# Two accumulating transfers in place of four behind each seven-product unit, and buffer pools of 34 and 34

## The chip, the cores and the metric

The kernel runs on one core of a Trainium2 chip. The metric is the device time of one execution in microseconds (us), the median of several runs. Names of engines: PE is TensorE (matmuls), DVE is VectorE, ACT is ScalarE, POOL is GpSimd, which here issues DMAs, and SP is SyncE, which issues the weight loads. PEld are TensorE's weight loads.

## The reference

One layer of an encoder on 512 tokens of width 2048, all in float32:

```
h = rmsnorm(x); proj = h @ w_in
attn   = mixture_of_dilations(q, k, v)          # 16 heads, three dilated windows
gla    = chunked gated linear attention, forward + backward, norm, swish gate
x = x + concat(attn, gla) @ w_out
h = rmsnorm(x)
x = x + (silu(h @ w_gate) * (h @ w_up)) @ w_down   # hidden width 5632
return rmsnorm(x) * final_norm_w
```

What matters here are the matrix products with `w_in` (its query and key columns), `w_gate` and `w_up`.

## The kernel before

Every float32 operand is cut into two parts, hi (a cast to fp32r) and lo (the difference to the original), and a product is the sum of hi·hi, hi·lo and lo·hi. The products with `w_gate` and `w_up` (class `Feed`, the feed-forward stage) and with the query and key columns of `w_in` (class `Front`, the front stage, which inherits from it) go by a scheme with seven products in place of eight for a 2 x 2 block product. A *unit* is 256 columns of one weight; `Feed` has 44 units (gate and up in turn), `Front` 8. A unit runs in four *pieces* (q = 0 to 3) of the contraction, and each piece needs:

- a raw weight tile, loaded by SyncE (`read`, L1366), at most three ahead;
- block sums of it on VectorE (`sums`, L1385 to L1387);
- two casts on ScalarE (`split`, L1398: one of 768 columns from the raw tile, one of 1024 from the sums) and two differences on VectorE (L1403);
- 28 matmuls on TensorE (`products`, L1480 and L1494) into seven banks of PSUM.

The pieces are prepared about one piece ahead: the loop `run` calls `split(i + 1)` ahead of `products(i)`. After the fourth piece `evac7` takes the seven banks m1, t2, t1, t3, m2, t4, b22 out of PSUM. The first halves are combined on VectorE into the tile c (L1514 and L1515, the names of the small helpers `add` and `sub`); the second halves are copied by ScalarE (L1520 to L1528) into r1, r2, r3, and after the addition at L1538 (which the profile shows at the helper's line, L1514, with 128x512 elements) GpSimd issues four DMAs that add them into c. The transfers overlap in c's columns, so the third and fourth wait until the first two have landed. `finish` then multiplies c on VectorE (L1578 for gate, L1585 for up, L1637 in the front stage), some pieces later. The first two units of `Feed` use another scheme (`evac`) without such transfers, so 42 + 8 units have them.

Buffers come from two pools: s2 with tiles of 512 columns (2 KB in each of 128 partitions) and s4 with tiles of 1024 columns. Each pool hands out the slot that was given back longest ago (`Slots`, a queue). Everything is given out when the program is built; at run time an instruction that writes a slot waits for the last users of that slot. On each engine the instructions run in the order in which the program lists them. `KEEP_X`, `KEEP_F` and `MOST_4` say how many operands go to which pool.

Of the kernel before, what the change touches and what calls it, by code (L numbers as in the profile page):

```python
# [15 lines left out]
F32 = mybir.dt.float32  # L16
# [3 lines left out]
OP = mybir.AluOpType  # L20
# [3 lines left out]
P = 128  # L24
# [9 lines left out]
BIG = 1e30  # L34
LINE = 1024
BIASW = 896
KEEP_X, KEEP_F, MOST_4 = 5, 2, 18

C_AQ, C_AK, C_AV = 0, 1024, 2048
C_GQ, C_GK, C_GV, C_GR, C_LR = 3072, 3584, 4096, 5120, 6144  # L40

N2 = 36
N4 = 33

# [66 lines left out]
def put(*slots):  # L113
    for s in slots:
        if s.home is not None:
            s.home.free.append(s.i)


def layer(nc, tc, x, attn_norm_w, w_in, rel_table, gw_f, gb_f, gw_b, gb_b, gla_norm_w, w_out,
# [3 lines left out]
    w_gate, w_up, w_down, out = w_gate[0], w_up[0], w_down[0], out[0]  # L123
    pe, act, dve, pool, sp = nc.tensor, nc.scalar, nc.vector, nc.gpsimd, nc.sync
    mm = pe.matmul

    with tc.manual_schedule(), \
# [4 lines left out]
            tc.tile_pool(name="ps", bufs=1, space=PSUM, reuse_waits="tile") as pp:  # L132
        s2 = Slots(p2, N2, 512, "a")
        s4 = Slots(p4, N4, 1024, "b")
        ps = Slots(pp, 8, 512, "ps")
# [44 lines left out]
        class Stream:  # L180
# [14 lines left out]
            def add(self, pieces):  # L195

                for segs in pieces:
                    self.pieces.append([segs, None])
                    for h in range(2):
                        self.halves.append([len(self.pieces) - 1, h, None, None])  # L200
# [1208 lines left out]
        class Feed(Blocks):  # L1409
# [100 lines left out]
            def evac7(self, u, banks):  # L1510


                a, z = slice(0, 256), slice(256, 512)
                add = lambda o, x_, y_: dve.tensor_tensor(o, x_, y_, op=OP.add)  # L1514
                sub = lambda o, x_, y_: dve.tensor_tensor(o, x_, y_, op=OP.subtract)  # L1515
                c_ = s4.get(F32, [P, 2, 512])
                c = c_.t.rearrange("p f t -> p (f t)")
                m1, t2, t1, t3, m2, t4, b22 = (b.t for b in banks)
                t, v, r1, r2, r3 = (s2.get() for _ in range(5))
                act.copy(t.t[:, a], m1[:, a])  # L1520
                act.copy(r3.t[:, a], t1[:, z])
                act.copy(r2.t[:, z], t1[:, z])
                act.copy(r3.t[:, z], t3[:, z])
                act.copy(r1.t[:, a], m2[:, z])
                act.copy(c[:, 512:768], t4[:, a])
                act.copy(r2.t[:, a], t4[:, z])  # L1526
                act.copy(c[:, 256:512], b22[:, a])
                act.copy(r1.t[:, z], b22[:, z])  # L1528
                add(t.t[:, a], t.t[:, a], m1[:, z])
                sub(t.t[:, z], t.t[:, a], t2[:, a])  # L1530
                sub(t.t[:, z], t.t[:, z], t2[:, z])
                add(v.t[:, a], t1[:, a], t.t[:, z])
                add(v.t[:, z], t3[:, a], t.t[:, z])
                add(c[:, 768:1024], t1[:, a], v.t[:, z])
                add(c[:, a], m2[:, a], t.t[:, a])
                put(*banks)
                yield
                add(c[:, 256:768], c[:, 256:768], v.t)  # L1538
                put(t, v)
                pool.dma_start(out=c[:, 0:512], in_=r1.t, accum_op=OP.add)  # L1540
                pool.dma_start(out=c[:, 512:1024], in_=r2.t, accum_op=OP.add)
                pool.dma_start(out=c[:, 256:768], in_=r3.t, accum_op=OP.add)
                pool.dma_start(out=c[:, 768:1024], in_=r3.t[:, z], accum_op=OP.add)
                put(r1, r2, r3)
                for _ in range(3 if u < len(self.units) - 2 else 7):
                    yield
                yield from self.finish(u, c_, c)
# [601 lines left out]
```

## Time and profile before

| | |
|---|---|
| time, median of 3 runs | 2184.84 us (2183.32 to 2185.92) |
| span of the profiled execution | 2184.5 us |
| busy PE / DVE / ACT / POOL | 99% / 81% / 55% / 16% |
| granted TensorE clock | 0.999 |
| TensorE's share of the chain that ended last | 87% |
| DMA | 397.81 MB, mean 182 GB/s |

The profile is of one execution. Its page lists busy time for each engine, groups of instructions by line, and DMA issues with the time to landing. In a row of a timeline stand the start, the duration, the engine, the line, the operation, the tiles written and read (a is s2, b is s4, ps a PSUM bank) and, in brackets, the time for which the engine was idle before, with what ended that. A row of waits gives the engine that waited, the one that released it, the total in us, how many times, and the longest.

### The profile page before, as it was taken

How to read it: one execution, taken by the hardware profiler on the slowest of the kernel's cores; microseconds unless marked ns; L12 is line 12 of the kernel's file. 1: busy time of each engine (PE TensorE's matmuls, PEld its weight loads, DVE VectorE, ACT ScalarE, POOL GpSimd, SP SyncE). 2: the span in 40 equal slices, each digit the busy share in tenths (PEclk: the TensorE clock that was granted, in tenths of full speed). 3: DMA queues.
4: the chain of work that ended last, by engine and by line, in shares of the span. 5: the costliest groups of instructions: out<-in, count | busy, mean ns of one | idle time of the engine just before them, and what ended most of it. 6: DMA issues, size and time to landing. Idle time of an engine off the chain costs nothing.

```text
span 2184.5 us, 34570 instructions
## 1 busy us (share of the span) xinstructions
PE 2163.5 (99%) x12618; PEld 1904.8 (87%) x12618; DVE 1770.9 (81%) x3072; ACT 1195.3 (55%) x2190; POOL 338.8 (16%) x474
## 2 busy tenths in 40 slices
PE   9999999999999999999999999999999999999998
PEld 7888778888888888988888888888888899999986
DVE  5699867776677557899999899998999888898885
ACT  7454456776654335555555555555555655555562
POOL 0012231110101110012212122121221220021300
PEclk9999999999999999999999999999999999999999
DMA  6367784543337873377767777767776975576982
GB/s 191 125 182 176 184 240 131 179 142 105 116 97 255 293 261 107 116 186 176 194 174 184 184 176 193 176 183 184 176 194 176 264 195 181 184 182 157 283 305 78
DMA packets 256856, 397.81 MB, mean 182 GB/s; under 512 B 18925, under 2 KB 154269, under 8 KB 256686
## 3 DMA queue, kind: packets, MB, share of 16 engines
q1 hardware_dynamic: 201406, 272.49, 39.1%
q0 software_dynamic: 54960, 122.58, 24.9%
q8 instruction: 99, 1.62, 0.3%
q14 instruction: 71, 0.58, 0.1%
q10 hardware_dynamic: 320, 0.53, 0.1%
HBM read 285.37 MB, written 64.29 MB: 160 GB/s over the span
## 4 chain that ended last, share of the span: by engine, by line
PE 87%; issue 6%; DMA 3%; DVE 2%; ACT 1%; POOL 0%; DVEq 0%; ACTq 0%; SPq 0%; POOLq 0%
PE ps L1494 26%; PE ps L1480 13%; PE ps L346 6%; PE ps L347 6%; PE ps L348 6%; PE ps L1850 5%; PE ps L1851 5%; PE ps L1849 5%; DMA b<-a 3%; PE ps L339 3%; PE ps L337 3%; PE ps L338 3%; PE ps L651 1%; PE ps L1075 1%; PE ps L619 1%
## 5 line engine op out<-in xcount | busy, mean ns | idle before, releaser
L1398 ACT CAST b<-b 128x768 fp32r<-128x768 f32 (+1 forms) x537 | 489.2, 945 | 337.4 <-DVE b L1403 150.0
L1403 DVE TENSOR_TENSOR b<-b,b 128x768 fp32r<-128x768 f32 (+1 forms) x537 | 564.0, 1084 | 33.9 <-ACT b L1398 21.9
L1494 PE MATMUL ps<-b,b 128*128 128x512 f32 x1552 | 451.2, 393 | 0.4 <-ACT b L1398 0.2
L1494 PE MATMUL ps<-a,b 128*128 128x512 f32 x1248 | 366.0, 394 | 3.3 <-DVE b L1514 3.3
L1494 PEld LDWEIGHTS ps<-b,b 128*128 128x128 f32 x1552 | 263.6, 189 | 30.6 <-ACT b L1398 0.7
L1480 PEld LDWEIGHTS ps<-b,b 128*128 128x128 f32 x1552 | 252.9, 190 | 36.0
L1480 PE MATMUL ps<-b,b 128*128 128x256 f32 x1552 | 275.9, 281 | 0.0
L1480 PEld LDWEIGHTS ps<-a,b 128*128 128x128 f32 x1248 | 208.0, 189 | 34.1 <-DVE b L1403 0.4
L1494 PEld LDWEIGHTS ps<-a,b 128*128 128x128 f32 x1248 | 207.3, 189 | 23.4 <-ACT a L1526 4.0
L1480 PE MATMUL ps<-a,b 128*128 128x256 f32 x1248 | 223.9, 281 | 0.0
L1385 DVE TENSOR_TENSOR b<-b 128x512 f32<-128x512 f32 x244 | 167.4, 686 | 20.1 <-DMA b<-in_w_down_dram 6.7
L1850 PE MATMUL ps<-b,b 128*128 128x256 f32 x624 | 176.9, 284 | 0.0
L1851 PE MATMUL ps<-b,b 128*128 128x256 f32 x624 | 176.9, 284 | 0.0
L1849 PE MATMUL ps<-b,b 128*128 128x256 f32 x624 | 176.9, 284 | 0.0
L346 PE MATMUL ps<-b,b 128*128 128x512 f32 x352 | 140.7, 400 | 2.0 <-ACT b L237 2.0
L347 PE MATMUL ps<-b,b 128*128 128x512 f32 x352 | 138.4, 393 | 0.9 <-DVE b L218 0.9
L348 PE MATMUL ps<-b,b 128*128 128x512 f32 x352 | 138.2, 392 | 0.0
L1851 PEld LDWEIGHTS ps<-b,b 128*128 128x128 f32 x624 | 119.9, 192 | 0.0
L1849 PEld LDWEIGHTS ps<-b,b 128*128 128x128 f32 x624 | 119.9, 192 | 0.0
L1850 PEld LDWEIGHTS ps<-b,b 128*128 128x128 f32 x624 | 119.9, 192 | 0.0
L218 DVE TENSOR_TENSOR b<-b,b 128x512 fp32r<-128x512 f32 x144 | 96.5, 687 | 24.0 <-ACT b L237 23.9
L1387 DVE TENSOR_TENSOR b<-b,b 128x256 f32<-128x256 f32 x244 | 103.8, 426 | 8.4
(294 smaller groups left out, 4352.2 us busy)
## 6 DMA issues: line engine op xcount, KB each, us to landing
b<-in_w_gate_dram SPq DMA_DIRECT2D x109, 512.0 KB, 4.1
b<-in_w_up_dram SPq DMA_DIRECT2D x88, 512.0 KB, 3.8
b<-in_w_down_dram SPq DMA_DIRECT2D x88, 512.0 KB, 6.6
b<-in_w_in_dram SPq DMA_DIRECT2D x78, 512.0 KB, 4.2
b<-a POOLq DMA_DIRECT2D x150, 256.0 KB, 4.5
b<-in_w_out_dram SPq DMA_DIRECT2D x32, 512.0 KB, 6.6
gd<-b POOLq DMA_DIRECT2D x22, 512.0 KB, 3.9
b<-gd SPq DMA_DIRECT2D x22, 512.0 KB, 5.7
```

Source lines behind the costliest of these rows:

```text
L346: mm(o, xh.t[:, c], wh.t[:, w], start=first and not on, stop=False, skip_group_check=on)
L347: mm(o, xh.t[:, c], wl.t[:, w], start=False, stop=False, skip_group_check=on)
L348: mm(o, xl.t[:, c], wh.t[:, w], start=False, stop=last, skip_group_check=on)
L1385: dve.tensor_tensor(s_[:, :, 0:2], r[:, :, 1:3], r[:, :, 0:1].to_broadcast(shape), op=OP.add)
L1387: dve.tensor_tensor(s_[:, :, 3], s_[:, :, 2], r[:, :, 3], op=OP.add)
L1398: act.copy(o, src)
L1403: dve.tensor_tensor(o, src, h, op=OP.subtract)
L1480: mm(o, wl, xh, start=False, stop=end, skip_group_check=True)
L1494: mm(o.rearrange("p (s t) -> p s t", s=2), wh, x_, start=first and p == 0, stop=False, skip_group_check=True)
L1849: mm(o, xh[:, t], wh, start=first and h == 0, stop=False, skip_group_check=True)
L1850: mm(o, xh[:, t], wl, start=False, stop=False, skip_group_check=True)
L1851: mm(o, xl[:, t], wh, start=False, stop=last, skip_group_check=True)
```

## The change

The copies of the second halves go into two s4 tiles, r with 1024 columns and g with 768, in place of three s2 tiles. r is added to all of c by one transfer and g to columns 256 to 1023 by a second, which waits for the first. For that the second half of t3 is copied twice into g by one instruction that reads it with a stride of zero. The pools change from 36 and 33 slots to 34 and 34 (the same memory), `KEEP_X` from 5 to 2 and `MOST_4` from 18 to 19. From L1520 on, lines of the changed kernel stand one lower or higher: the two transfers are its L1541 and L1542, and the stages behind them are one line earlier.

```diff
-KEEP_X, KEEP_F, MOST_4 = 5, 2, 18
+KEEP_X, KEEP_F, MOST_4 = 2, 2, 19
...
-N2 = 36
-N4 = 33
+N2 = 34
+N4 = 34
...
                 m1, t2, t1, t3, m2, t4, b22 = (b.t for b in banks)
-                t, v, r1, r2, r3 = (s2.get() for _ in range(5))
+                t, v = s2.get(), s2.get()
+                r, g = s4.get(), s4.get(F32, [P, 768])
                 act.copy(t.t[:, a], m1[:, a])
-                act.copy(r3.t[:, a], t1[:, z])
-                act.copy(r2.t[:, z], t1[:, z])
-                act.copy(r3.t[:, z], t3[:, z])
-                act.copy(r1.t[:, a], m2[:, z])
+                act.copy(g.t[:, 0:256], t1[:, z])
+                act.copy(r.t[:, 768:1024], t1[:, z])
+                act.copy(g.t[:, 256:768].rearrange("p (i c) -> p i c", i=2), t3[:, None, z].to_broadcast([P, 2, 256]))
+                act.copy(r.t[:, 0:256], m2[:, z])
                 act.copy(c[:, 512:768], t4[:, a])
-                act.copy(r2.t[:, a], t4[:, z])
+                act.copy(r.t[:, 512:768], t4[:, z])
                 act.copy(c[:, 256:512], b22[:, a])
-                act.copy(r1.t[:, z], b22[:, z])
+                act.copy(r.t[:, 256:512], b22[:, z])
...
                 add(c[:, 256:768], c[:, 256:768], v.t)
                 put(t, v)
-                pool.dma_start(out=c[:, 0:512], in_=r1.t, accum_op=OP.add)
-                pool.dma_start(out=c[:, 512:1024], in_=r2.t, accum_op=OP.add)
-                pool.dma_start(out=c[:, 256:768], in_=r3.t, accum_op=OP.add)
-                pool.dma_start(out=c[:, 768:1024], in_=r3.t[:, z], accum_op=OP.add)
-                put(r1, r2, r3)
+                pool.dma_start(out=c, in_=r.t, accum_op=OP.add)
+                pool.dma_start(out=c[:, 256:1024], in_=g.t, accum_op=OP.add)
+                put(r, g)
```

## The prediction

> **What bounds the kernel now.** I read the page first, then the stretches of the feed-forward stage, then the waits of TensorE, and then the timelines of VectorE, ScalarE and GpSimd through two units.
>
> ```profile
> span 2184.5 us, 34570 instructions
> PE 2163.5 (99%) x12618; PEld 1904.8 (87%) x12618; DVE 1770.9 (81%) x3072; ACT 1195.3 (55%) x2190; POOL 338.8 (16%) x474
> 1000.00:1019.50 19.50, 19.50 (x114) 17.12 (x113) 17.07 (x27) 10.10 (x18) 4.02 (x5) 1.00 0.77 211
> 1019.50:1039.00 19.50, 19.50 (x114) 17.12 (x113) 17.99 (x29) 11.35 (x20) 3.51 (x4) 1.00 0.65 154
> PE ps L1494 <- DVE b L1514: 3.3, 4, 1.8
> ```
>
> TensorE is busy for 99% of the span, and in the two stretches (two units, a gate and an up unit) it has no pause; so the kernel runs at TensorE's pace. The columns after the length are PE, PEld, DVE, ACT and POOL busy. VectorE is second: 17.07 and 17.99 of 19.50 us, so it can be stopped for about 1.5 to 2.4 us in a unit before it sets the pace itself. The last row is TensorE's longest kind of wait in the front stage (125 to 288 us): 3.3 us for banks that the evacuation frees late. That is what a better evacuation could win.
>
> **The unit's loop.** The change touches the four accumulating transfers. Their rows for one unit, then their landing times over the 41 units between 920 and 1710 us, and the count of units in the front stage:
>
> ```profile
> 1004.32 0.86 POOL L1540 DMA_DIRECT2D b<-a  x1 [3.83 <-PE ps L1480]
> 1004.87 1.22 POOL L1541 DMA_DIRECT2D b<-a  x1
> 1010.60 0.87 POOL L1542 DMA_DIRECT2D b<-a  x1 [4.51 <-issue]
> 1011.14 1.21 POOL L1543 DMA_DIRECT2D b<-a  x1
> ...
> L1540 POOL DMA_DIRECT2D b<-a x41: 857/862/905, 927.7 to 1706.3; - x41
> ...
> L1541 POOL DMA_DIRECT2D b<-a x41: 1188/1200/1234, 928.3 to 1706.9; - x41
> DMA to landing us min/median/max: 4.3/5.3/11.1
> ...
> L1543 POOL DMA_DIRECT2D b<-a x40: 872/1208/1230, 934.1 to 1694.3; - x40
> DMA to landing us min/median/max: 3.9/5.4/7.1
> ...
> L1540 POOL DMA_DIRECT2D b<-a x7: 862/862/899, 135.6 to 259.1; - x7
> ```
>
> From first to last issue, a unit takes (1706.3 - 927.7) / 40 = 19.47 us, a pair 38.93; in the front stage (259.1 - 135.6) / 6 = 20.58 us.
>
> Before, r1, r2, r3 lie in s2 slots that only the next unit's evacuation takes again. After, r and g lie in s4, from which every cast (L1398), difference (L1403) and weight load takes its buffers in turn. The listing of the changed program's instructions shows who gets them. Its instruction order on TensorE, VectorE, ScalarE and SyncE is as before; only the tiles and the waits differ:
>
> ```
> 205 L1541 DMACopy b0_833_9821<-b2_834_9824 128x1024
> 206 L1542 DMACopy b0_833_9821<-b28_835_9825 128x768
> 1004 L1398 TensorCopy b2_849_9942<-b11_832_9791 128x768 [waits DMAHW0_49,DMASW5_49]
> 1005 L1398 TensorCopy b28_850_9943<-b14_842_9896 128x1024 [waits DMASW6_49,DVE_49]
> 208 L1542 DMACopy b8_860_10020<-b1_862_10024 128x768 [waits DMASW7_49]
> 1448 L1385 TensorTensor b21_875_10138<-b17_868_10054 128x2x256 [waits DMAHW6_49,DMASW7_49]
> 1023 L1398 TensorCopy b1_876_10142<-b31_859_9990 128x768 [waits DMAHW5_49,DMASW0_49]
> ```
>
> The number after b is the slot. Slot 28 was g of one unit; the second cast for piece 3 of the next unit writes it, so that cast waits until g has landed. In the other kind of unit (g in slot 1) it is the first cast. These two kinds take turns through the whole feed-forward stage; the front stage has the second kind in all but its last unit. VectorE's difference reads the cast, and behind it in VectorE's order stand the rest of the casts' differences, the evacuation, and the addition after which the next r may start. This is a closed loop, and its time is the unit's time once it exceeds 19.47 us.
>
> **Its length, from rows.** The addition, the difference that will wait, and the next addition, for the two kinds and for the front stage; the two casts; and VectorE's waits for others between 1009.6 and 1042.6 us and, last row, between 181.4 and 195.6 us:
>
> ```profile
> 1003.07 0.69 DVE L1514 TENSOR_TENSOR b<-b,a 128x512 f32<-128x512 f32 x1
> 1009.59 1.22 DVE L1403 TENSOR_TENSOR b<-b,b 128x1024 fp32r<-128x1024 f32 x1
> 1022.57 0.69 DVE L1514 TENSOR_TENSOR b<-b,a 128x512 f32<-128x512 f32 x1
> 1028.22 0.95 DVE L1403 TENSOR_TENSOR b<-b,b 128x768 fp32r<-128x768 f32 x1
> 1042.70 0.69 DVE L1514 TENSOR_TENSOR b<-b,a 128x512 f32<-128x512 f32 x1
> ...
> 181.40 0.95 DVE L1403 TENSOR_TENSOR b<-b,b 128x768 fp32r<-128x768 f32 x1
> 195.63 0.69 DVE L1514 TENSOR_TENSOR b<-b,a 128x512 f32<-128x512 f32 x1
> ...
> 1008.71 0.84 ACT L1398 CAST b<-b 128x768 fp32r<-128x768 f32 x1 [1.23 <-PE ps L1480]
> 1009.70 1.05 ACT L1398 CAST b<-b 128x1024 fp32r<-128x1024 f32 x1 [0.16 <-DVE b L1403]
> ...
> DVE a L1514 <- ACT a L1520: 1.7, 1, 1.7
> DVE a L1514 <- PE ps L1480: 0.5, 2, 0.3
> DVE b L1585 <- DMA b<-a: 0.5, 1, 0.5
> DVE b L1403 <- PE ps L1480: 0.2, 1, 0.2
> ...
> DVE a L1514 <- ACT a L1522: 1.2, 1, 1.2
> ```
>
> *The transfers.* No row shows an accumulating transfer of 1024 or 768 columns, so they are bounded by the pairs with the same bytes. Pair one, from first issue to last landing: 0.55 (1004.87 - 1004.32) + 5.3 = 5.85 us in the median, 0.55 + 4.3 = 4.85 at best. Pair two: 0.55 + 5.4 = 5.95, or 4.45. Between them lies one step of GpSimd, which I take from addition's end to issue: 1004.32 - 1003.76 = 0.56. So the chain is 12.36 us if the merged transfers take what the pairs' medians take. At best it is 9.86, less the two second issues of 0.55, 8.76. Nothing speaks for an end (less contention at a slower pace, but twice the bytes in each packet), so I take the middle, 10.56. With the step ahead of r, g lands G = 11.12 us after the addition ends.
>
> *VectorE behind it.* First kind: from 1009.59 to the next addition's end at 1023.26, 13.67 us; second kind: 1028.22 to 1043.39, 15.17. Of these 28.84 us, 2.9 were waits for others, which a late VectorE no longer meets: 25.94 remain. With the cast that waits ahead of each (1.05 and 0.84) a pair takes 2G + 27.83 = 50.07 us in place of 38.93. G lands 5.3 and 6.2 us after the difference's old start (5.83 and 4.96 us after the addition), far over VectorE's room.
>
> *The sum.* The feed-forward stage has 42 such units; the first is not held up, so 41 are, 20.5 pairs: 20.5 x 11.14 = 228 us. The front stage: 14.92 us (181.40 to 196.32) - 1.2 + 0.84 + 11.12 = 25.68 in place of 20.58, in 7 of its 8 units: 7 x 5.10 = 36 us. Total 2184.5 + 228 + 36 = **2448 us**. The profiled execution's 2184.5 stands within 0.4 us of the median of the runs shown (2184.84), so no correction is due. At a chain of 8.76 the same sum gives 2362, at 12.36 it gives 2535.
>
> *The rest, priced at nothing.* A hundred fewer issues by GpSimd (0.86 to 1.22 us each) shorten no chain, since GpSimd is 16% busy. The front stage's 3.3 us of bank waits are inside the old 20.58 and so gone already in the new period. One copy out of a bank is 512 columns wide in place of 256:
>
> ```profile
> L1524 ACT COPY a<-ps 128x256 f32<-128x256 f32 x2 | 0.7, 373 | 0.6 <-PE ps L1480 0.6
> L1582 ACT ACTIVATE b<-b 128x512 f32<-128x512 f32 x2 | 1.2, 636 | 0.0
> ```
>
> At most 0.636 - 0.373 = 0.26 us, hidden by ScalarE's waits while VectorE is late; without that cover 50 x 0.26 = 13 us. KEEP_X and MOST_4 move operands between pools without adding instructions. Weight loads in the front stage now take the slot of a stored result and wait for that store, with SyncE's later loads queued behind. They have to be there for block sums, which wait for r's landing anyway; without this cover, some 1 us in each of 7 units.
>
> **The rivals.**
>
> *Merging pays more.* Plain transfers of 512 KB issued by GpSimd:
>
> ```profile
> gd<-b POOLq DMA_DIRECT2D x22, 512.0 KB, 3.9
> qkd<-b POOLq DMA_DIRECT2D x8, 512.0 KB, 3.1
> ```
>
> If a merged transfer landed in 3.9 or 3.1 us like these, the chain would be 8.36 or 6.76 us, the pair 45.67 or 42.47, the front unit 23.48 or 21.88, and the time 2343 or 2266: about 2305. Against it: in the best pair, 512 KB accumulated took 4.85. The page "DMA: Bandwidth & Descriptors" of the Trainium skill (section "Anatomy of one DMA") speaks for it: it fits a GpSimd transfer as 2.0 us plus bytes at 436 GB/s, an estimate of 3.2 and 2.9 us here, and so 2261 us.
>
> *TensorE restarts slowly.* In the new loop it would stand still some 25.0 - 19.5 = 5.5 us in each unit. At the kernel's start, between 6 and 16 us, the same matmul took longer than on average:
>
> ```profile
> L346 PE MATMUL ps<-b,b 128*128 128x512 f32 x5 | 3.3, 663 | 2.0 <-ACT b L237 2.0
> L346 PE MATMUL ps<-b,b 128*128 128x512 f32 x352 | 140.7, 400 | 2.0 <-ACT b L237 2.0
> ```
>
> Some eight slow ones by 0.26 us after each pause are 2.1 us; half would reach the evacuation, 1 us in 48 units: 2496. Against it: TensorE has the 5.5 us to make it up, and the granted clock in the stretches read 1.00. The page "TensorE: Matmul & The Clock Gate" (Part 1) of the Trainium skill says that an idle window of about 3.4 us halves the clock until a busy one has passed; no pause in this trace is that long (the longest in the row above is 1.8).
>
> *Faster.* If the slots came round late enough, the casts would not wait; only the front stage's 3.3 us would go: 2181. It decides at 2G + 27.83 = 38.93, G = 5.55, a chain under 4.99 us. Pair one alone needed 4.85 at best, so two transfers cannot fit.
>
> **How the numbers follow.** The loop as summed 0.76, a shorter chain 0.12, slow restarts 0.08, faster 0.03, and 0.01 for no change by casts that wait without holding VectorE. Slower than by 0.2% (4.4 us, about what a measurement of this kernel can tell) are the first three: 0.96. The range takes in the sum's bounds and the upper half of the shorter chain: 2335 to 2535.
>
> **What would show it.** Right: ScalarE at L1398 waits for the DMA of b, 3 to 8 us in every unit; VectorE at L1403 waits for it; TensorE is busy near 80% between 930 and 1700 us; first issues lie 25 us apart. The chain's term is read from L1541's and L1542's landings. Wrong: casts that start as before, or landings near 3.1 us, which put the time near 2266.

## The result, and the profile after

The changed kernel took **2498.08 us** in the median (2490.17 to 2502.15), the kernel before 2184.84 (2183.32 to 2185.92): a ratio of **1.143**, with a 95% interval of 1.1416 to 1.144. The forecast was 2448 us, with a range of 2335 to 2535.

First the page of the changed kernel: its span, the busy times, the granted clock in 40 slices (9 is 90% or more), and of its DMA issues those of r, g and the store of gate's result, with KB each and the median us to landing.

```profile
span 2497.6 us, 34239 instructions
PE 2285.8 (92%) x12618; PEld 1967.8 (79%) x12618; DVE 1772.1 (71%) x3072; ACT 1196.2 (48%) x2190; POOL 249.6 (10%) x374
...
PEclk9998899999999999989889898898888999999999
...
b<-b POOLq DMA_DIRECT2D x50, 512.0 KB, 6.2
b<-b POOLq DMA_DIRECT2D x50, 384.0 KB, 4.8
...
gd<-b POOLq DMA_DIRECT2D x22, 512.0 KB, 5.4
```

VectorE and ScalarE did the same work as before (1770.9 and 1195.3 us), and GpSimd less (338.8 before). TensorE shows 122 us more of busy time with the same instructions: matmuls that ran slower, of which more below. The rest of the 313 us is idle time, and the waits of the changed kernel say for what:

```profile
ACT b L1398 <- DMA b<-b: 513.4, 68, 13.4
POOL b L1541 <- DVE b L1385: 381.8, 25, 19.1
...
POOL b L1542 <- DMA b<-b: 287.1, 49, 9.3
DVE b L1403 <- ACT b L1398: 271.4, 85, 6.5
PE ps L1494 <- ACT b L1398: 177.0, 58, 7.6
...
DVE b L1385 <- DMA b<-b: 73.5, 24, 5.1
```

Read them as a ring: GpSimd starts g's transfer (L1542) when r has landed, ScalarE's casts wait for the transfers (`DMA b<-b`), VectorE waits for the casts, and GpSimd waits for VectorE before it can issue the next r. (The profile infers who released a wait: for r it mostly names L1385 or L1398, but in the timeline below each r is issued 0.6 us behind the end of the addition, L1514.) That TensorE's 177 us of waiting for casts are a consequence, two of the runs below test. Before, the casts' longest wait was for VectorE, and TensorE's waits were a few us.

Two units of the changed kernel in its timelines, a few instructions of GpSimd, ScalarE and VectorE (start, duration, engine, line, operation, tiles, and the idle time before it with what ended that); the rows between them are left out:

```profile
1493.49 0.68 DVE L1514 TENSOR_TENSOR b<-b,a 128x512 f32<-128x512 f32 x1
1494.81 0.86 POOL L1541 DMA_DIRECT2D b<-b  x1 [3.89 <-ACT b L1398]
1502.71 0.83 ACT L1398 CAST b<-b 128x768 fp32r<-128x768 f32 x1 [8.05 <-DMA b<-b]
1502.97 0.87 POOL L1542 DMA_DIRECT2D b<-b  x1 [7.31 <-DMA b<-b]
1507.02 2.73 ACT L1398 CAST b<-b 128x1024 fp32r<-128x1024 f32 x3 [3.47 <-DMA b<-b]
1508.09 3.23 DVE L1403 TENSOR_TENSOR b<-b,b 128x1024 fp32r<-128x1024 f32 x3 [3.56 <-ACT b L1398]
1512.47 0.59 ACT L1524 COPY b<-ps 128x512 f32<-128x512 f32 x1 [0.34 <-PE ps L1480]
1518.89 0.69 DVE L1514 TENSOR_TENSOR b<-b,a 128x512 f32<-128x512 f32 x1
1520.19 0.87 POOL L1541 DMA_DIRECT2D b<-b  x1 [16.35 <-DVE b L1385]
1525.85 0.69 DVE L1385 TENSOR_TENSOR b<-b 128x512 f32<-128x512 f32 x1 [2.75 <-DMA b<-b]
1526.11 0.86 POOL L1542 DMA_DIRECT2D b<-b  x1 [5.05 <-DMA b<-b]
1530.12 3.46 ACT L1398 CAST b<-b 128x768 fp32r<-128x768 f32 x4 [9.33 <-DMA b<-b]
...
1544.25 0.69 DVE L1514 TENSOR_TENSOR b<-b,a 128x512 f32<-128x512 f32 x1
```

Both kinds of unit are there, in turn. In the first, a cast starts when r has landed (1502.71) and the next when g has (1507.02). In the second, the block sums start when r has landed (1525.85) and a cast when g has (1530.12). From addition to addition it is 25.40 and 25.36 us here.

The changed kernel's line L1541, over the feed-forward stage (41 units) and over the front stage (7 units): issue durations in ns (least, median, most), first and last start, and the time to landing.

```profile
L1541 POOL DMA_DIRECT2D b<-b x41: 860/862/900, 978.5 to 2013.8; - x41
...
DMA to landing us min/median/max: 5.1/6.1/9.9
...
L1541 POOL DMA_DIRECT2D b<-b x7: 856/862/899, 137.0 to 302.7; - x7
...
DMA to landing us min/median/max: 5.5/6.3/8.0
```

A feed-forward unit takes (2013.8 - 978.5) / 40 = 25.88 us in place of 19.47, a front unit (302.7 - 137.0) / 6 = 27.62 in place of 20.58. 41 x 6.41 + 7 x 7.04 = 312 us, and the spans differ by 2497.6 - 2184.5 = 313.1. So the loss is all in these units.

### The profile page after: what moved, and what is told of

It reads as the page before. It is cut to its first block, busy times and chain, and to the rows that moved or that the text cites. A ratio compares the mean times of both kernels' runs of the same rounds, so it can differ in the third digit from the quotient of the medians.

```text
span 2497.6 us, 34239 instructions
## 1 busy us (share of the span) xinstructions
PE 2285.8 (92%) x12618; PEld 1967.8 (79%) x12618; DVE 1772.1 (71%) x3072; ACT 1196.2 (48%) x2190; POOL 249.6 (10%) x374
## 4 chain that ended last, share of the span: by engine, by line
PE 25%; DMA 12%; DVE 10%; issue 8%; ACT 3%; POOL 1%; DVEq 0%; ACTq 0%; POOLq 0%
DMA b<-b 12%; PE ps L1494 4%; PE ps L1849 4%; PE ps L1848 4%; PE ps L1850 4%; DVE b L1403 4%; ACT b L1398 3%; PE ps L1480 2%; DVE b L1385 1%; PE ps L346 1%; PE ps L347 1%; PE ps L348 1%; DVE b L1514 1%; DVE a L1514 1%; DVE b L1584 1%
## 5 line engine op out<-in xcount | busy, mean ns | idle before, releaser
L1398 ACT CAST b<-b 128x768 fp32r<-128x768 f32 (+1 forms) x537 | 479.8, 942 | 738.4 <-DMA b<-b 513.4
L1403 DVE TENSOR_TENSOR b<-b,b 128x768 fp32r<-128x768 f32 (+1 forms) x537 | 564.4, 1085 | 274.9 <-ACT b L1398 271.4
L1494 PE MATMUL ps<-a,b 128*128 128x512 f32 x1248 | 422.2, 443 | 145.6 <-ACT b L1398 145.6
L1494 PE MATMUL ps<-b,b 128*128 128x512 f32 x1552 | 459.9, 399 | 31.4 <-ACT b L1398 31.4
L1494 PEld LDWEIGHTS ps<-a,b 128*128 128x128 f32 x1248 | 235.6, 215 | 175.9 <-ACT b L1398 156.4
L1494 PEld LDWEIGHTS ps<-b,b 128*128 128x128 f32 x1552 | 269.4, 193 | 62.3 <-ACT b L1398 33.0
L1480 PEld LDWEIGHTS ps<-a,b 128*128 128x128 f32 x1248 | 233.1, 216 | 88.7 <-DVE b L1403 54.4
L1480 PEld LDWEIGHTS ps<-b,b 128*128 128x128 f32 x1552 | 256.5, 193 | 40.6 <-DVE b L1403 3.8
L1480 PE MATMUL ps<-b,b 128*128 128x256 f32 x1552 | 280.4, 284 | 0.5 <-DVE b L1403 0.5
L1480 PE MATMUL ps<-a,b 128*128 128x256 f32 x1248 | 261.7, 314 | 11.9 <-DVE b L1403 10.9
L1385 DVE TENSOR_TENSOR b<-b 128x512 f32<-128x512 f32 x244 | 167.7, 687 | 124.6 <-DMA b<-b 73.5
L1849 PE MATMUL ps<-b,b 128*128 128x256 f32 x640 | 181.3, 283 | 0.0
L1850 PE MATMUL ps<-b,b 128*128 128x256 f32 x640 | 181.3, 283 | 0.0
L1848 PE MATMUL ps<-b,b 128*128 128x256 f32 x640 | 181.3, 283 | 0.0
L346 PE MATMUL ps<-b,b 128*128 128x512 f32 x380 | 153.4, 404 | 9.1 <-ACT b L237 9.1
L347 PE MATMUL ps<-b,b 128*128 128x512 f32 x380 | 150.5, 396 | 0.9 <-DVE b L218 0.9
L348 PE MATMUL ps<-b,b 128*128 128x512 f32 x380 | 150.2, 395 | 0.0
L1848 PEld LDWEIGHTS ps<-b,b 128*128 128x128 f32 x640 | 123.0, 192 | 0.0
L1849 PEld LDWEIGHTS ps<-b,b 128*128 128x128 f32 x640 | 123.0, 192 | 0.0
L1850 PEld LDWEIGHTS ps<-b,b 128*128 128x128 f32 x640 | 123.0, 192 | 0.0
L218 DVE TENSOR_TENSOR b<-b,b 128x512 fp32r<-128x512 f32 x154 | 103.4, 686 | 19.6 <-ACT b L237 19.6
```

The lines of the kernel that those rows point to most:

```text
L346: mm(o, xh.t[:, c], wh.t[:, w], start=first and not on, stop=False, skip_group_check=on)
L347: mm(o, xh.t[:, c], wl.t[:, w], start=False, stop=False, skip_group_check=on)
L348: mm(o, xl.t[:, c], wh.t[:, w], start=False, stop=last, skip_group_check=on)
L1385: dve.tensor_tensor(s_[:, :, 0:2], r[:, :, 1:3], r[:, :, 0:1].to_broadcast(shape), op=OP.add)
L1398: act.copy(o, src)
L1403: dve.tensor_tensor(o, src, h, op=OP.subtract)
```

## Experiments

Each ran beside the kernel before, which had medians of 2185.55 to 2186.20 us in these comparisons. *Theory* is the loop: casts and sums that take r's and g's buffers wait for the landing, and in-order engines carry the delay round to the next r. A figure in the expectations, 11.53 us from r's issue to g's landing, is a mean over 41 units; the last of them, behind which other work runs, is an outlier, and without it the mean is 11.37.

**Give r and g back two steps later.** The transfers stay two; only the place at which the buffers return to the pool moves, so that other tiles take them later.

```diff
-                put(r, g)
-                for _ in range(3 if u < len(self.units) - 2 else 7):
+                for n in range(3 if u < len(self.units) - 2 else 7):
+                    if n == 2:
+                        put(r, g)
                     yield
```

> The changed kernel with r and g given back two steps of the evacuation later (two pieces later), so that the free queue hands their slots out only after g has landed; the transfers stay as they are. Slot theory (the time comes from casts that wait for g's landing because they were given its slot): every such wait goes and the time comes back to 2178 to 2192 us, TensorE near 99% busy in the stage. Transfer theory (the two large accumulating transfers themselves slow the core, by contention or by a late result): they are all still there, so 2450 to 2500 us.

Measured: 2200.42 us, ratio 1.0063 (1.0048 to 1.0078). r's issues and landings in that run, and then two of the waits that are left in it:

```profile
L1541 POOL DMA_DIRECT2D b<-b x41: 860/862/900, 926.5 to 1720.2; - x41
...
DMA to landing us min/median/max: 4.6/5.7/9.9
```

```profile
PE ps L1494 <- DVE b L1514: 12.1, 15, 1.8
...
ACT b L1522 <- DMA b<-b: 46.5, 16, 4.5
```

298 of the 313 us are gone, with the merged transfers and the pools of 34 and 34 in place; r lands only little sooner. The place of giving back is the cause. The 8 us above the expected range are not all explained; the two waits shown, for banks and for a slot that a transfer still reads, are among what is left.

**One step later.** The same edit with `n == 1`.

> As the changed kernel, with r and g given back one step later: g's slot now goes to a cast of the next unit's first piece (in place of its predecessor's fourth), whose difference stands some 2.2 us (first kind of unit) and 3.5 us (second kind and front stage) later in VectorE's order. Slot theory, by the same loop sum with the chain as measured after the change (11.4 us in the mean, GpSimd's step 0.28): pair 2 x 11.68 + 1.89 + 20.15 = 45.4 us in place of 38.93, front unit 23.2 in place of 20.58, so 2184 + 133 + 18 = 2335 us (2310 to 2365). If a wait for g cost the same wherever it stands: 2498. If only the fourth piece's wait mattered: 2185.

Measured: 2338.36 us, ratio 1.0702 (1.0679 to 1.0724). r's issues in that run, and its longest wait of the casts:

```profile
L1541 POOL DMA_DIRECT2D b<-b x41: 860/864/902, 952.8 to 1862.0; - x41
```

```profile
ACT b L1398 <- DMA b<-b: 262.6, 66, 8.6
```

(1862.0 - 952.8) / 40 = 22.73 us for a unit, so 45.46 for a pair where the loop's sum gave 45.4. The loss shrinks in steps with the place of giving back, as the theory has it.

**Leave g's transfer out.** The result then lacks g's addend; the casts still wait for r.

```diff
                 pool.dma_start(out=c, in_=r.t, accum_op=OP.add)
-                pool.dma_start(out=c[:, 256:1024], in_=g.t, accum_op=OP.add)
```

> The changed kernel with g's transfer left out (its 768 columns are missing from c); the copies into g stay, and r's transfer and all slots stay. Slot theory: g's slots have no late reader, only r's remain; r lands 6.4 us after the addition. First kind of unit: the fourth piece's first difference comes 2.3 us late, of which VectorE's 2.0 us of waits hide most; second kind: block sums 2.95 us late, 1.0 hidden; front 1.75 net. 20.5 x 2.25 + 7 x 1.75 = 58, so 2243 us (2220 to 2265). Transfer theory: with 384 of 896 KB gone, 43% of the loss goes: 2364 us.

Measured: 2292.21 us, ratio 1.0487 (1.0472 to 1.0503): between the two forecasts, and above the theory's range. r's issues and landings in that run:

```profile
L1541 POOL DMA_DIRECT2D b<-b x41: 853/864/897, 949.4 to 1819.2; - x41
...
DMA to landing us min/median/max: 4.7/7.2/9.4
```

The theory had r land 6.4 us after the addition ends. In the mean it was 7.33 here and 8.17 in the front stage (worked out from the trace), 0.93 and 1.77 later. With that the expectation's sum gives a pair 2.25 + 2 x 0.93 = 4.11 us more than before and a front unit 1.75 + 1.77 = 3.52: 20.5 x 4.11 + 7 x 3.52 = 109 us, and 2184.5 + 109 = 2293.5 where the span is 2294.5. That was worked out afterwards. This made the landing time the open question.

**Less work for TensorE.** In the middle pieces of each seven-product unit 28 half-wide matmuls (lo·hi) are left out. The expectation speaks of the 42 units of the feed-forward stage, but the front stage takes `products` from the same class, so all 50 units lose them: the page counts 11218 matmuls in place of 12618, 1400 fewer.

```diff
-                            rest.append((o[:, 0:256], wl, xh, end))
+                            if not together:
+                                rest.append((o[:, 0:256], wl, xh, end))
```

> The changed kernel with the lo-hi matmuls of the two middle pieces left out in the 42 seven-product units of the feed-forward stage (that part of the product is missing): 28 matmuls of 256 columns fewer in a unit, 3.4 us of TensorE's work at its full pace. If VectorE's loop through g sets the unit's time, TensorE only waits longer: 2480 to 2500 us. If TensorE's slow restarts (granted clock 0.944) set it, or any part of its work is in the loop, the time falls by up to 42 x 3.4 = 143: 2355 us.

Measured: 2558.78 us, ratio 1.1703 (1.1685 to 1.172). Less work, and 61 us *more* than the changed kernel, outside what either side had expected. r's issues (L1542 there) and landings in that run, and TensorE's wait:

```profile
L1542 POOL DMA_DIRECT2D b<-b x41: 860/864/900, 982.4 to 2076.1; - x41
...
DMA to landing us min/median/max: 5.8/8.2/9.9
```

```profile
PE ps L1494 <- ACT b L1398: 389.7, 70, 10.5
```

TensorE only waits longer, so its work does not set the pace. What changed is the landing: r takes 8.2 us. More weight loads ran beside it: in the 6 us behind r's issue their queue moved 1050 KB in the mean of the 41 units, against 823 KB in the changed kernel (worked out from the traces). Why the loads moved there is not shown; slots that TensorE gives up sooner, so that loads into them start sooner, would do it.

**More work for TensorE.** The same 28 matmuls are issued twice, again in all 50 units (14018 matmuls); the kernel then computes another result.

```diff
                     for o, wl, xh, end in rest:
+                        if together:
+                            mm(o, wl, xh, start=False, stop=False, skip_group_check=True)
                         mm(o, wl, xh, start=False, stop=end, skip_group_check=True)
```

> The changed kernel with more work for TensorE: each of the 28 half-wide matmuls (256 columns) that the middle pieces of a feed-forward unit put last is issued twice (the output is another one). At 0.12 us each that is 3.4 us per unit. Theory (the loop through the slots sets the pace, TensorE has slack): nothing is added, the period stays at 25 to 26 us, 2498 us (2440 to 2515); with less TensorE work the transfers had landed later and the time had grown by 60 us, so a fall below 2498 would fit. Rival (TensorE's own work, or its slow restarts, set the pace): 41 x 3.4 = 139 us more, 2637 us (2600 to 2660).

Measured: 2520.58 us, ratio 1.1526 (1.1506 to 1.1545). At the expectation's 0.12 us each, the 1400 matmuls are 168 us of work (its 139 us counted 41 units of the feed-forward stage alone), and they cost 22. That is 6 us above the theory's range and 79 below the rival's. r's issues (L1543 there) and landings in that run, and TensorE's wait:

```profile
L1543 POOL DMA_DIRECT2D b<-b x41: 860/862/900, 977.5 to 2028.8; - x41
...
DMA to landing us min/median/max: 4.5/6.9/9.5
```

```profile
PE ps L1496 <- ACT b L1398: 66.3, 28, 3.6
```

The extra work went into TensorE's waits for casts (66.3 us are left of 177.0). What it cost came by the landing: 6.9 us for r, and in the feed-forward stage 0.39 us more from the addition to g's landing (the table below).

**Four transfers in the changed kernel's buffers.**

```diff
-                pool.dma_start(out=c, in_=r.t, accum_op=OP.add)
-                pool.dma_start(out=c[:, 256:1024], in_=g.t, accum_op=OP.add)
+                pool.dma_start(out=c[:, 0:512], in_=r.t[:, 0:512], accum_op=OP.add)
+                pool.dma_start(out=c[:, 512:1024], in_=r.t[:, 512:1024], accum_op=OP.add)
+                pool.dma_start(out=c[:, 256:768], in_=g.t[:, 0:512], accum_op=OP.add)
+                pool.dma_start(out=c[:, 768:1024], in_=g.t[:, 512:768], accum_op=OP.add)
```

> The changed kernel with its buffers (r and g among the slots that casts and sums reuse, given back at once), but with the four accumulating transfers of before (512 columns each) instead of two. Theory (the loop through the slots): the time hangs on the time from the first issue to the last landing; in the feed-forward stage of the kernel before, four transfers took 12.39 us on average and the two of the changed kernel 11.53 us, so each unit gets about 0.9 us longer: 2498 + 48 x 0.9 = 2541 us (2510 to 2580). Rival (merged transfers are what is slow): with four transfers the kernel goes back to 2185 to 2300 us.

Measured: 2563.48 us, ratio 1.1727 (1.1702 to 1.1752). The first issues of that run's units:

```profile
L1541 POOL DMA_DIRECT2D b<-b x41: 860/862/905, 983.0 to 2068.4; - x41
```

So the merging is not what is slow: in the same loop, four transfers cost 65 us more than two, (2068.4 - 983.0) / 40 = 27.14 us for a unit against 25.88.

**More traffic on the DMA engines.** Behind each weight load of these units (and of the first two of the feed-forward stage), SyncE also copies half of the tile to a place that nothing reads. This asks what makes r and g land later than the sum had it.

```diff
+        ex, extra = dr.tile([256, P, 512], F32, name="ex"), []
...
                              in_=w[k * P:(k + n_kt) * P, col:col + n].rearrange("(k p) c -> p k c", p=P))
+                if not isinstance(self, Down):
+                    sp.dma_start(out=ex[len(extra)].rearrange("p (k c) -> p k c", k=2),
+                                 in_=w[k * P:(k + 2) * P, col:col + n].rearrange("(k p) c -> p k c", p=P))
+                    extra.append(i)
```

> The changed kernel, and SyncE issues behind each weight load of the seven-product units (and of their first two) a copy of half of that weight tile (256 KB) to a place in the chip's memory that nothing reads. No instruction of TensorE, VectorE, ScalarE or GpSimd changes. It asks why the two transfers of r and g took longer from first issue to last landing (11.53 us on average in the feed-forward stage) than the 10.56 us of the sum. Theory (the weight loads that are under way take a share of the DMA engines): in the changed kernel r's landing grew by about 0.45 us per 100 KB of weight loads in the 6 us behind its issue, 824 KB on average; with 250 to 400 KB more there, r lands 1 to 2 us later and g 0.5 to 1 us later, the unit gets as much longer, and the time is 2498 + 48 x (1.5 to 3) = 2570 to 2640 us. Rival (the landing times are the transfers' own, and the weight loads only happen to go along): landings stay at 6.1 and 4.8 us and the time at 2498 us, 2485 to 2515.

Measured: 2578.68 us, ratio 1.1795 (1.1775 to 1.1814), within the theory's range. Its issues and landings of r (L1546 there) and of g:

```profile
L1546 POOL DMA_DIRECT2D b<-b x41: 862/865/902, 992.0 to 2093.0; - x41
...
DMA to landing us min/median/max: 5.3/7.0/10.3
...
L1547 POOL DMA_DIRECT2D b<-b x41: 862/865/881, 998.2 to 2103.6; - x41
...
DMA to landing us min/median/max: 3.9/5.4/7.8
```

In the median r lands 0.9 us later than in the changed kernel (1 to 2 were expected) and g 0.6 us later, and nothing else was changed but the traffic. So transfers beside them do slow r and g. How much of their 6.1 and 4.8 us is owed to the weight loads of the changed kernel itself, no run took away.

**Buffers of their own.** r and g in two tiles that no cast and no sum takes; to make room, pools of 32 and 33, with `KEEP_X` and `MOST_4` as before.

```diff
+        sr = Slots(prg, 1, 1024, "r")
+        sg = Slots(prg, 1, 768, "g")
...
-                r, g = s4.get(), s4.get(F32, [P, 768])
+                r, g = sr.get(), sg.get()
```

> The two merged transfers, with r and g in two tiles of their own (4 KB and 3 KB per partition, used by every unit in turn, taken by no cast and no sum); pools of 32 and 33 buffers, and the pools' other settings as before the change, to make room. Theory (only the reuse of r's and g's buffers by casts and sums costs): the loop is gone, 2180 to 2215 us, with 2178 to 2190 if one pair of half-size buffers fewer than before costs nothing. Rival (merged transfers are slow by themselves): 2400 us or more.

Measured: 2215.65 us, ratio 1.0139 (1.0122 to 1.0156), 0.65 us above the theory's range and far below the rival's. A wait of ScalarE's in that run, and one of VectorE's behind it:

```profile
ACT g L1525 <- DMA b<-g: 96.9, 30, 9.1
...
DVE a L1517 <- ACT r L1526: 47.9, 30, 8.4
```

The big loop is gone, but a small one has come: with one g for all units, the next evacuation's copy into g (L1525 there) waits for the last unit's transfer out of it, 96.9 us in all, and VectorE for the copies.

**Late giving back with the old pools.** `put(r, g)` three steps later, and pools, `KEEP_X` and `MOST_4` as in the kernel before.

```diff
-KEEP_X, KEEP_F, MOST_4 = 2, 2, 19
+KEEP_X, KEEP_F, MOST_4 = 5, 2, 18
-N2 = 34
-N4 = 34
+N2 = 36
+N4 = 33
...
-                put(r, g)
                 for _ in range(3 if u < len(self.units) - 2 else 7):
                     yield
+                put(r, g)
```

> The two merged transfers, r and g among the slots as in the changed kernel but given back three steps later, and the pools and their settings as before the change (36 and 33 buffers). Theory (the time of giving back decides): no loop, 2180 to 2215 us; with one slot of the large kind fewer than in the run that gave them back two steps later (2200 us), the casts wait for the slots somewhat more, so rather 2190 to 2215. Rival (34 large buffers are needed for r and g): 2250 us or more.

Measured: 2197.45 us, ratio 1.0053 (1.0038 to 1.0068), as the theory had it. The casts' longest wait in it is for VectorE again, as in the kernel before (150.0 us there):

```profile
ACT b L1398 <- DVE b L1403: 181.0, 72, 6.1
```

This has the lowest median of the versions with two transfers (2200.42 for the one above is close), and it still loses about 11 us to the kernel before. None of the runs beats that one.

**All runs in one line of arithmetic.** For each run with the giving back as in the changed kernel and both r and g: G, from the end of the addition to g's landing, and the period from addition to addition, both means over 40 units of the feed-forward stage, worked out from the trace.

| kernel | G, us | period, us | period less G |
|---|---|---|---|
| changed | 12.05 | 25.88 | 13.83 |
| more work for TensorE | 12.44 | 26.28 | 13.84 |
| four transfers | 13.23 | 27.14 | 13.91 |
| less work for TensorE | 13.46 | 27.34 | 13.88 |
| more DMA traffic | 13.63 | 27.52 | 13.90 |

The period is G and a constant; whatever was done to TensorE, to the transfers or to the traffic moved G, and the constant by less than 0.1 us. It holds unit by unit: in the changed kernel the difference is 14.8 to 14.9 us in every unit of one kind and 12.6 to 13.2 in the other, while G goes from 10.1 to 14.6. The prediction's constant was 27.83 / 2 = 13.92. In the kernel before the same difference is 6.64, and G does not count there.

## Why the prediction was right, step by step

*The loop.* Right, as the runs with a later giving back and the table show. The two kinds of units take turns as listed.

*VectorE behind it.* 13.92 us forecast in the feed-forward stage, 13.83 measured; 14.92 - 1.2 + 0.84 = 14.56 forecast in the front stage, 14.83 measured. So taking VectorE's waits for others out of the sum was right.

*The transfers: the term that was mis-sized.* The sum took 10.56 us for the chain and 0.56 ahead of it: G = 11.12. Measured were 11.37 and 0.68 in the feed-forward stage (12.05), 12.16 and 0.63 in the front stage (12.79). Inside the chain GpSimd's step from r's landing to g's issue took 0.30 us where 0.56 was priced, so the two landings were under-priced by more than the chain was: 11.07 us in place of 10.00 in the feed-forward stage. The step that failed is the sentence that nothing speaks for an end of the bounds. The slower pace did not thin the traffic beside r: in the 6 us behind r's issue the weight loads' queue moved 823 KB in the mean of the 41 units, and behind the first issue in the kernel before 719 KB; in the front stage 905 KB against 542 (worked out from the traces). That slots come free together, and weight loads start with them, is a likely reason; no run tested it. While r was under way, the loads' queue and GpSimd's queue each had 48% of the DMA engines' time in the mean of the 41 units. The stretch between 1494 and 1502 us shows one r that landed late, after some 8 us (packets, MB, share of the 16 engines); there the loads' queue, q1, had more than half:

```profile
q1 hardware_dynamic: 1130, 1.35, 51.7%
q0 software_dynamic: 251, 0.90, 46.3%
```

The Trainium skill (page "DMA: Bandwidth & Descriptors", section "Queues, rings and completion order") says that a DMA engine serves the queues that have work in turn, a packet at a time. The shares here and the run with more traffic fit that, but do not show the order of the packets. In time the miss is 41 x (25.88 - 25.03) + 7 x (27.62 - 25.68) = 35 + 14 = 49 us, which is the difference between 2448 and the span of 2497.6: nothing outside these units was missed.

*Merging pays more.* Wrong as forecast: landings of 6.2 and 4.8 us in the median, not 3.9 or 3.1. The estimate from the Trainium skill (page "DMA: Bandwidth & Descriptors", section "Anatomy of one DMA"), 3.2 and 2.9 us, stands under every landing seen (at least 5.1 us for r over the whole run, 3.9 for g). The two transfers were still faster than four in the same place, by about 1.2 us per unit of the feed-forward stage.

*TensorE restarts slowly.* Its 2496 us stand nearest to the result, but by chance. The slow matmuls are there, in TensorE's timeline of the changed kernel (pairs of matmuls), and so is the lower clock, in two stretches (length, then busy PE, PEld, DVE, ACT and POOL, then the granted clock, the DMA share and GB/s):

```profile
1503.60 0.73 PE L1494 MATMUL ps<-a,b 128*128 128x512 f32 x2 [1.49 <-ACT b L1398]
1504.59 0.50 PE L1480 MATMUL ps<-a,b 128*128 128x256 f32 x2 [0.26 <-DVE b L1403]
1508.11 1.22 PE L1494 MATMUL ps<-a,b 128*128 128x512 f32 x2 [3.02 <-ACT b L1398]
...
1512.27 0.62 PE L1494 MATMUL ps<-b,b 128*128 128x512 f32 x2
...
1501.70:1505.10 3.40, 1.65 (x8) 0.80 (x6) 0.96 (x1) 0.83 (x1) 0.87 (x1) 1.00 0.94 304
1505.20:1511.90 6.70, 3.75 (x10) 2.74 (x11) 3.71 (x5) 3.41 (x6) 0.00 (x0) 0.50 0.19 35
```

At 1508.11 a pair takes 1.22 us, and 4 us later 0.62 again. By the profile the granted clock halved at about 1505.1 us, where the pause of 3.02 us began, and so not because of that pause: in the 3.4 us ahead TensorE had been busy for 1.65, with no pause longer than 1.49. It stayed at 0.50 until about 1512, 3.8 us after TensorE took up work. The Trainium skill (page "TensorE: Matmul & The Clock Gate", Part 1) puts the idle window that halves the clock at about 3.4 us, and the busy window that brings it back at about the same. The way back fits that here; the halving does not, since the 3.4 us ahead of it were half busy. But the forecast that half of the delay reaches the evacuation did not hold: the constant in the table, which holds all that lies between a landing and the next addition, is no longer than its sum without slow matmuls, and 168 us more of matmuls cost only 22. The 122 us of added busy time are spent inside the waiting.

*Faster* was out of reach by 6.4 us: it needed a chain under 4.99, and 11.37 was measured.

*What was priced at nothing.* Fewer issues by GpSimd shortened no chain that counts, other than the chain of transfers itself. The wide copy took 0.59 us (L1524 above) where narrow ones take 0.37, 0.22 more, covered. Weight loads behind the front stage's stores had at most the 14.83 - 14.56 = 0.27 us of that constant.

*What would show it.* Issues were 25.9 us apart where 25 was forecast. TensorE's busy share between 930 and 1700 us was 664.11 / 770 = 86%, above the "near 80%", since slow matmuls count as busy:

```profile
930.00:1700.00 770.00, 664.11 (x3463) 558.57 (x3462) 540.64 (x839) 323.19 (x541) 56.87 (x71) 0.90 0.51 136
```

The casts' waits for the transfers were 513.4 us in all, some 10 in each of 49 units, not 3 to 8: ScalarE, too, is idle through nearly the whole chain. VectorE's waits at L1403 came as forecast (271.4 us).

## What to carry to other kernels

A buffer that a DMA still reads is not free when the program gives it back; in a pool that hands out the slot given back longest ago, ask which instruction gets it next, and what stands behind that on an engine that works in order. If that leads round to the DMA's own start, the period is the DMA's landing time and a constant, the work from the landing to the next start; here neither more nor less work for TensorE, the busiest engine, changed that constant. Give the buffer back later, or let it have users that come a whole round later. Price a DMA in such a loop at its landing beside the traffic that will run with it: here the chain took 11.37 and 12.16 us in the two stages, between the middle (10.56) and the upper bound (12.36).

## What the runs showed of the hardware

- Less work for TensorE made the kernel slower (2498 to 2559 us): more weight loads ran in the 6 us behind r's issue (1050 KB against 823), and its landing went from 6.1 to 8.2 us.
- A plain store of 512 KB, which the prediction took for 3.9 us from the kernel before, landed in 5.4 us in the changed kernel; accumulating 512 KB from buffer to buffer took 6.2 there, at other moments of the unit.
- One transfer of 512 KB and one of 384 KB took less from first issue to last landing (11.37 us) than the same bytes in four (12.55 us).
- In the stretch shown, TensorE's granted clock halved after 3.4 us in which TensorE was busy for 1.65 and never paused for longer than 1.49, and came back 3.8 us after TensorE took up work again.
